# A float32 hybrid decoder layer on one core: planner margins, the gate between attention pairs, the place of the weight loads and of the softplus's rectifier

## The chip, the cores and the metric

The kernel runs on one core of one Trainium2 chip. The metric is the time of one execution on the device in microseconds (us). The core has a matrix engine (TensorE, in the rows PE for matmuls and PEld for weight loads into the array), VectorE (DVE), ScalarE (ACT), GpSimd (POOL) and SyncE (SP), whose queue here issues nearly all DMA transfers.

## The reference

One pre-norm layer with 512 tokens of width 2048, in float32. `h = RMSNorm(x)`; one projection `h @ w_in` gives three groups of heads:

- a: RWKV-7 time mixing, 12 heads of 64: a recurrence over time with data-dependent decay (sigmoids, exponentials, a normalised key), then a group norm and a bonus term.
- b: causal pooling over windows of 2, 4, 8, 16, a 128x128 map and a scale for each of four groups.
- c: stick-breaking attention, 12 heads of 64. Queries and keys are RMS-normalised; `z = q k^T`; the weight of a key is `exp(logsigmoid(z) + sum over the later keys before the query of logsigmoid(-z))`; output is weights times values.

Each branch is multiplied by a SiLU gate from the same projection; the concatenation goes through `w_out` and is added to `x`.

## The kernel before

**Precision and the main stream.** Every big product is made of three matmuls: both operands are split into a rounded part and a rest (`hh`, `hl` for the activations, `wh`, `wl` for the weights), and `three` issues hh*wh, hh*wl and hl*wh into one PSUM tile. The projection has 57 column tiles of 128; the first three are done while the inputs arrive, and `project(n)` does each of the other 54 in two halves of 24 matmuls into a bank named `pj` (two of them). Tile order for pair p of heads: cq, ck, cv, cg (attention), k, r of the next pair, v, ga (RWKV), and four times pu, pg (pooling) at the end. Then the output projection runs into banks named `oacc`, four column blocks of eight halves.

**Weights.** `stream` lists the 140 half tiles of weights. `weights(i)` calls `fetch(i)` and `fetch(i + 1)`; a fetch allocates `raw` (two buffers), issues its DMA on SP, casts it on ACT to `wh` (three buffers) and subtracts on DVE to `wl` (two buffers). It does so under a raised priority (`AHEAD`, 300 places).

**The rest is fill-in.** `rwkv(p)`, `attention(p)` and `pooling(g)` are generators. After every matmul of the main stream `pump` resumes each generator whose due time has passed on the clock of `Pace`, a planner with its own costs that is advanced by each matmul (`pace.now`). `need(tiles, tag, margin)` is due at margin (default `MARGIN` = 2.5) after the later of two things: the planner's ready time of the tiles, and the moment when a PSUM bank of that tag (three `g` banks) has been read. `soon` is due 1.5 before the tiles are ready. So a larger margin puts a step's matmuls behind more matmuls of the main stream. What is written so is a program order; when the program is built, a scheduler gives every engine a fixed queue, by priority (program place, less the raise) among what it holds to be ready, and semaphores do the waiting on the chip.

**Attention of a pair.** `attention(p)` waits for the end of pair p-1 (`done[("att", p - 1)]`), then for cq and ck: square, split, a block sum on TensorE (`qm`), a Newton rsqrt, the scaled q and k. For each head and three groups of key blocks it makes `z` on TensorE, copies it to `w`, masks it on POOL, and forms the softplus: `n` = ln(1 + exp(-|w|)) by three ACT steps, `m` = relu(w) by a fourth (`m` has one buffer), a reversed scan over n + m on DVE, a subtraction and an exponential into `w`. Then come the transposes `wT` of the weights into g banks, their copies `wt` on ACT, and the products `o` into a g bank that is kept until all three column groups are in. `emit_rstd` makes the norm of `x` (bank `rb`), which the first finished tiles wait for.

Of the kernel before, what the change touches and what calls it, by code (L numbers as in the profile page):

```python
# [13 lines left out]
P = 128  # L14
# [203 lines left out]
def hybrid_trunk_kernel(ctx: ExitStack, tc: tile.TileContext, x, xT, w_in, w_out, vecs, consts, up_w, pool_w, out):  # L218
# [21 lines left out]
    def name(s):  # L240
        uid[0] += 1
        return f"{s}_{uid[0]}"
# [17 lines left out]
    def gb(s="g"):  # L260
        return bank("g", s)
# [96 lines left out]
    def emit_rstd():  # L358
        rt = cp.tile([P, 3, 4], F32, name="rt")
        ms, y0, t = rt[:, 0, :], rt[:, 1, :], rt[:, 2, :]  # L360
        dve.tensor_tensor(ms, xsum[:, 0, :], xsum[:, 1, :], ALU.add)
        dve.tensor_scalar(ms, ms, 1.0 / D, RMS_EPS, ALU.mult, ALU.add)
        act.activation(y0, ms, AF.Ln)
        act.activation(y0, y0, AF.Exp, scale=-0.5)
        dve.tensor_tensor(t, y0, y0, ALU.mult)
        dve.tensor_tensor(t, ms, t, ALU.mult)
        dve.tensor_scalar(t, t, -0.5, 1.5, ALU.mult, ALU.add)
        dve.tensor_tensor(y0, y0, t, ALU.mult)
        dg = tmp("dg")
        for i in range(4):  # L370
            dve.tensor_scalar(dg[:, i * P:(i + 1) * P], ident, y0[:, i:i + 1], None, ALU.mult)
        rb = gb("rb")
        pe.matmul(rb, ones_c, dg, start=True, stop=True)
        dve.tensor_copy(out=rstd, in_=rb)


# [34 lines left out]
    def soon(*tiles):  # L411
        return need(*tiles, margin=-1.5)
# [29 lines left out]

    HK = KT // 2

    def split_weights(src):
        raw = wp.tile([P, HK * P], F32, tag="raw", bufs=2, name=name("raw"))
        dma(out=raw, in_=src)
        wh = wp.tile([P, HK * P], F32R, tag="wh", bufs=3, name=name("wh"))
        wl = wp.tile([P, HK * P], F32R, tag="wl", name=name("wl"))
        act.copy(out=wh, in_=raw)  # L450
        dve.tensor_tensor(wl, raw, wh.bitcast(F32), ALU.subtract)
        return wh, wl
# [19 lines left out]
    def fetch(i):  # L472
        if i < len(stream) and i not in fetched:
            with tc.high_priority(offset=AHEAD if i > 1 else 60):
                fetched[i] = split_weights(stream[i])

    def weights(i):
        fetch(i)
        fetch(i + 1)
        return fetched.pop(i)  # L480

    def project(n):
# [71 lines left out]
    def rwkv(p):  # L554
# [18 lines left out]
        mm(av, uph[:, P:2 * P], ad2, True, False)  # L573
        mm(av, upl[:, P:2 * P], ad2, False, True)
        a = sigmoid(av, bias=nvec[:, 6 + p:7 + p])
        yield need(*sqp, tag="g")
        ss = gb("ss")
        block_sum(ss, bone_r, sqp)
        rn = sq
# [233 lines left out]


    def attention(p):
        while p > 0 and not done.get(("att", p - 1)):
            yield None
        qk = []
        for kind, gain, slot in (("cq", nvec[:, 12:13], "aq"), ("ck", vec[:, V_KN:V_KN + 1], "ak")):
            while (kind, p) not in got:  # L820
                yield None
            raw = got.pop((kind, p))
            dst = scratch(slot, kind)
            sq = tmp("qs")
            act.activation(sq, raw, AF.Square)
            sqp = split(sq)
            yield need(*sqp, tag="g")
            ms = gb("qm")
            block_sum(ms, bmean_r, sqp)
            y0, t = newton_rsqrt(ms, RMS_EPS, eps_rms, sq)  # L830
            dve.scalar_tensor_tensor(raw, raw, gain, y0, ALU.mult, ALU.mult)
            dve.tensor_tensor(dst, raw, t, ALU.mult)
            qk.append(dst)
# [3 lines left out]
        act.copy(out=kr, in_=k)  # L837
        klo = tmpr("klo")
        dve.tensor_tensor(klo, k, kr.bitcast(F32), ALU.subtract)
        head = []  # L840
        for h in range(2):
            s = slice(h * HD, (h + 1) * HD)
            other = hi if h == 0 else lo
            q2 = ap.tile([P, T], F32R, tag="q2", name=name("q2"))
            k2 = ap.tile([P, T], F32R, tag="k2", name=name("k2"))
            act.copy(out=q2[s, :], in_=q[s, :])
            dve.tensor_tensor(q2[other, :], q[s, :], q2[s, :].bitcast(F32), ALU.subtract)
            act.copy(out=k2[s, :], in_=k[s, :])
            act.copy(out=k2[other, :], in_=k[s, :])
            kl2 = ap.tile([P, T], F32R, tag="kl2", name=name("kl2"))  # L850
            pool.tensor_copy(out=kl2[s, :], in_=klo[s, :])
            pool.tensor_copy(out=kl2[other, :], in_=klo[s, :])
            blocks = {}
            for segs, width in ((((3, 0),), 512), (((2, 0), (0, 384)), 512), (((1, 0),), 256)):
                yield need(q2, k2, kl2, tag="g")
                z = gb("z")
                for i, off in segs:
                    mm(z[:, off:off + (i + 1) * P], q2[:, i * P:(i + 1) * P], k2[:, 0:(i + 1) * P], True, False)
                    mm(z[:, off:off + (i + 1) * P], q2[:, i * P:(i + 1) * P], kl2[:, 0:(i + 1) * P], False, True)

                d0 = segs[0][0] * P
                nd = len(segs)
                pat = [[0, nd], [-1, P]] if nd > 1 else [[-1, P]]
                diag = lambda t: t[:, d0:d0 + nd * P].rearrange("p (a t) -> p a t", a=nd) if nd > 1 else t[:, d0:d0 + P]
                w = ap.tile([P, width], F32, tag=f"w{segs[0][0]}{h}", name=name("w"))
                act.copy(out=w, in_=z[:, 0:width])
                pool.affine_select(out=diag(w), in_=diag(w), pattern=pat, compare_op=ALU.is_gt, fill=-1e5, base=0, channel_multiplier=1)

                n = ap.tile([P, 512], F32, tag="n", bufs=2, name=name("n"))[:, 0:width]
                m = ap.tile([P, 512], F32, tag="m", bufs=1, name=name("m"))[:, 0:width]  # L870
                act.activation(n, w, AF.Abs)
                act.activation(n, n, AF.Exp, scale=-1.0)
                act.activation(n, n, AF.Ln, bias=1.0)
                act.activation(m, w, AF.Relu)
                yield soon(n, m)
                for i, off in segs:
                    sg = slice(off, off + (i + 1) * P)
                    dve.tensor_tensor_scan(n[:, sg][:, ::-1], n[:, sg][:, ::-1], m[:, sg][:, ::-1], 0.0, ALU.add, ALU.add)
                dve.tensor_tensor(w, w, n, ALU.subtract)
                act.activation(w, w, AF.Exp)  # L880
                for i, off in segs:
                    for j in range(i + 1):
                        blocks[(i, j)] = w[:, off + j * P:off + (j + 1) * P]
            head.append(blocks)
            if h == 0:
                while ("cv", p) not in got:
                    yield None
                vs = got.pop(("cv", p))
                yield need(vs, tag="g", margin=MARGIN + 2.0)
                vt = ap.tile([P, 4, P], F32, tag="vt", name=name("vt"))  # L890
                vps = gb("vps")
                for j in range(4):
                    transpose(vps[:, j * P:(j + 1) * P], vs[:, j * P:(j + 1) * P])
                act.copy(out=vt, in_=vps.rearrange("p (j c) -> p j c", j=4))

        o = None
        for js, width in (((0,), 512), ((1, 3), 512), ((2,), 256)):
            parts = []
            for h in range(2):
                yield need(*head[h].values(), tag="g", margin=MARGIN + 2.0)  # L900
                tps = gb("wT")
                pos = {}
                off = 0
                for j in js:
                    pos[j] = slice(off, off + T - j * P)
                    for i in range(j, 4):
                        transpose(tps[:, off:off + P], head[h][(i, j)])
                        off += P
                home = {(0, 0): "q2", (0, 1): "k2", (1, 0): "kl2", (2, 0): "q2", (2, 1): "k2"}.get((js[0], h))
                wt = ap.tile([P, T], F32, tag=home, name=name("wt"))[:, 0:width] if home else tmp("wt", width)  # L910
                act.copy(out=wt, in_=tps[:, 0:width])
                parts.append(wt)
            yield need(*parts, vt, tag="g" if o is None else None)
            if o is None:
                o = gb("o")
            for j in js:
                for h, s in ((0, lo), (1, hi)):
                    mm(o[s, j * P:T], vt[:, j, s], parts[h][:, pos[j]], j == 0, j == 2)
# [104 lines left out]

    def begin():
        yield need(xsum, tag="g")
        emit_rstd()
        for n in range(NFIRST):
            finish(n, first[n])

# [134 lines left out]
```

## Time and profile before

| | us |
|---|---|
| median of three runs (range) | 1008.57 (1006.39 to 1008.71) |
| the profiled execution, time | 1007.96 |
| the profiled execution, span from first to last instruction | 1006.1 |
| matmul busy in the span | 978.3 |
| weight loads into the array, busy | 786.9 |
| VectorE busy | 662.2 |
| ScalarE busy | 511.6 |
| projection with fill-in, from 42.6 to 825.1 | 782.5 |
| output projection, from 825.1 to the end | 181.0 |

The engines' busy times overlap. Matmuls are pipelined and their ends are modelled: a 128x512 matmul is shown as some 0.39 to 0.40 us long, while the next one starts 0.22 to 0.23 us after it.

### The profile page before, as it was taken

Reading aid. Unit: us, or ns where it says so; the run is one execution under the profiler, and the core shown is the slowest. Engines: PE = TensorE matmul, PEld = TensorE weight load, DVE = VectorE, ACT = ScalarE, POOL = GpSimd, SP = SyncE. Lnnn points to the kernel's source line nnn. Section 1 sums busy time; section 2 is a strip of 40 time slices with the busy share of each in tenths; the row PEclk is TensorE's granted clock in tenths of the full one; section 3 lists DMA queues with packets and bytes.
Section 4 is the critical chain, followed back from the end, with each engine's and each line's share of the span. In section 5 each row is a group of like instructions: output and inputs, shape, how many; then the busy total and the mean of one; then the engine's idle time right before and its main releaser. Section 6 shows DMA issues by size and latency. Waiting matters only on the chain. (4 is left out here: it accounts for less than half of the span.)

```text
span 1006.1 us, 13872 instructions
## 1 busy us (share of the span) xinstructions
PE 978.3 (97%) x5132; PEld 786.9 (78%) x5132; DVE 662.2 (66%) x1249; ACT 511.6 (51%) x838; POOL 140.5 (14%) x204
## 2 busy tenths in 40 slices
PE   8999999999899998999999999999999999999998
PEld 7867876888678886788768887788867888888886
DVE  5369784888849885697947979398864666323232
ACT  5656654756556654647546565466552245221210
POOL 0131211121120302112111111203211010000000
PEclk9999999999999999999999999999999999999999
DMA  9622322132321313223131222313232248624241
GB/s 337 216 90 76 103 85 90 63 111 68 105 84 58 114 65 106 79 84 95 64 121 64 90 89 80 105 63 110 72 106 79 98 145 281 219 87 147 93 138 63
DMA packets 62210, 109.17 MB, mean 109 GB/s; under 512 B 29760, under 2 KB 31168, under 8 KB 62144
## 3 DMA queue, kind: packets, MB, share of 16 engines
q1 hardware_dynamic: 62144, 108.30, 32.1%
q8 instruction: 40, 0.66, 0.3%
q14 instruction: 26, 0.21, 0.1%
HBM read 98.84 MB, written 9.44 MB: 108 GB/s over the span
## 5 line engine op out<-in xcount | busy, mean ns | idle before, releaser
L380 PE MATMUL pj<-hh,wl 128*128 128x512 f32 x864 | 343.7, 398 | 7.8 <-DVE wl L212 7.5
L380 PE MATMUL pj<-hh,wh 128*128 128x512 f32 x864 | 345.8, 400 | 0.1
L380 PE MATMUL pj<-hl,wh 128*128 128x512 f32 x864 | 343.4, 398 | 0.0
L212 DVE TENSOR_TENSOR wl<-raw,wh 128x1024 fp32r<-128x1024 f32 x140 | 174.4, 1246 | 174.6 <-PE oacc L380 86.1
L212 ACT CAST wh<-raw 128x1024 fp32r<-128x1024 f32 x140 | 146.4, 1046 | 205.7 <-PE oacc L380 95.2
L380 PEld LDWEIGHTS pj<-hh,wl 128*128 128x128 f32 x864 | 162.8, 188 | 45.7 <-DVE wl L212 12.4
L380 PEld LDWEIGHTS pj<-hh,wh 128*128 128x128 f32 x864 | 162.8, 188 | 33.6 <-issue 1.8
L380 PEld LDWEIGHTS pj<-hl,wh 128*128 128x128 f32 x864 | 163.0, 189 | 32.6 <-issue 2.2
L380 PE MATMUL oacc<-wl,yh 128*128 128x512 f32 x256 | 100.1, 391 | 0.0
L380 PE MATMUL oacc<-wh,yh 128*128 128x512 f32 x256 | 99.8, 390 | 0.0
L380 PE MATMUL oacc<-wh,yl 128*128 128x512 f32 x256 | 99.7, 390 | 0.0
L212 POOL TENSOR_SCALAR e<-e 128x512 f32<-128x512 f32 x28 | 45.2, 1614 | 197.4 <-ACT e L212 179.4
L380 PEld LDWEIGHTS oacc<-wh,yl 128*128 128x128 f32 x256 | 48.1, 188 | 10.3 <-issue 0.2
L380 PEld LDWEIGHTS oacc<-wl,yh 128*128 128x128 f32 x256 | 48.1, 188 | 10.2 <-issue 0.2
L380 PEld LDWEIGHTS oacc<-wh,yh 128*128 128x128 f32 x256 | 48.1, 188 | 10.0 <-DVE u L212 0.2
L212 POOL TENSOR_TENSOR d<-u 128x512 f32<-128x512 f32 x25 | 29.4, 1176 | 149.3 <-DVE xblk L212 67.6
L212 DVE TENSOR_TENSOR pr<-xblk,nblk 128x60 f32<-128x60 f32 (+8 forms) x180 | 46.5, 258 | 5.0
L212 ACT ACTIVATE e<-e 128x512 f32<-128x512 f32 x50 | 31.5, 630 | 35.7 <-POOL e L212 35.3
L212 DVE TENSOR_TENSOR_SCAN n<-n,m 128x512 f32<-128x512 f32 (+3 forms) x48 | 43.8, 923 | 7.5 <-ACT n L212 7.5
L212 DVE TENSOR_TENSOR xblk<-xblk,pr 128x60 f32<-128x60 f32 (+8 forms) x180 | 39.3, 218 | 5.0
L212 POOL CAST kl<-klo 64x512 fp32r<-64x512 f32 x24 | 19.2, 802 | 150.4 <-DVE klo L212 134.9
L212 ACT ACTIVATE n<-n 128x512 f32<-128x512 f32 (+1 forms) x72 | 39.6, 551 | 0.4
(203 smaller groups left out, 1227.5 us busy)
## 6 DMA issues: line engine op xcount, KB each, us to landing
raw<-in_w_in SPq DMA_DIRECT2D x108, 512.0 KB, 3.4
raw<-in_w_out SPq DMA_DIRECT2D x32, 512.0 KB, 3.4
lt<-in_x SPq DMA_DIRECT2D x8, 512.0 KB
xr<-in_x SPq DMA_DIRECT2D x16, 256.0 KB, 5.5
out<-xr SPq DMA_DIRECT2D x16, 256.0 KB, 4.1
yin<-yd SPq DMA_DIRECT2D x14, 256.0 KB, 4.6
fr<-in_w_in SPq DMA_DIRECT2D x12, 256.0 KB, 6.9
nblk<-s SPq DMA_DIRECT2D x24, 128.0 KB, 3.4
```

The costliest lines, as they stand in the source:

```text
L212: return call(*args, **kw)
L380: pe.matmul(o, lhsT, rhs, start=start, stop=stop)
```

## The change

Nothing is computed differently and no instruction is added or removed; some are written down at other places in the program, and some waits of generators are due later. In the diff below:

- `emit_rstd` becomes a generator: its matmul waits for `dg` with a margin of 4.5, and is counted by the planner.
- The block sum of the first pair's key norm (`ss`) is due 3.0 later; that of each query and key norm (`qm`) 1.5 later; the transposes `wT` 2.0 later (6.5 for 4.5); the products `o` 1.5 later (4.0 for 2.5).
- `weights(i)` also issues the DMA of `raw` for i + 2; the cast and the subtraction stay in the fetch.
- `attention(p)` begins when the score part of pair p-1 is done, and waits for the whole of pair p-1 only ahead of its own scores.
- `m` = relu(w) is written after the wait `soon(n)`, just ahead of the scan.

```diff
@@ emit_rstd
         dg = tmp("dg")
         for i in range(4):
             dve.tensor_scalar(dg[:, i * P:(i + 1) * P], ident, y0[:, i:i + 1], None, ALU.mult)
+        yield need(dg, tag="g", margin=MARGIN + 2.0)
         rb = gb("rb")
-        pe.matmul(rb, ones_c, dg, start=True, stop=True)
+        mm(rb, ones_c, dg)
         dve.tensor_copy(out=rstd, in_=rb)
@@ weights
-    def split_weights(src):
-        raw = wp.tile([P, HK * P], F32, tag="raw", bufs=2, name=name("raw"))
-        dma(out=raw, in_=src)
+    raws = {}
+
+    def load_weights(i):
+        if i < len(stream) and i not in raws and i not in fetched:
+            raws[i] = wp.tile([P, HK * P], F32, tag="raw", bufs=2, name=name("raw"))
+            dma(out=raws[i], in_=stream[i])
+
+    def split_weights(i):
+        load_weights(i)
+        raw = raws.pop(i)
         wh = wp.tile([P, HK * P], F32R, tag="wh", bufs=3, name=name("wh"))
...
-                fetched[i] = split_weights(stream[i])
+                fetched[i] = split_weights(i)
 
     def weights(i):
         fetch(i)
         fetch(i + 1)
+        with tc.high_priority(offset=AHEAD):
+            load_weights(i + 2)
         return fetched.pop(i)
@@ rwkv
-        yield need(*sqp, tag="g")
+        yield need(*sqp, tag="g", margin=MARGIN + (3.0 if p == 0 else 0.0))
         ss = gb("ss")
@@ attention
-        while p > 0 and not done.get(("att", p - 1)):
+        while p > 0 and not done.get(("scores", p - 1)):
             yield None
...
-            yield need(*sqp, tag="g")
+            yield need(*sqp, tag="g", margin=MARGIN + 1.5)
             ms = gb("qm")
...
         dve.tensor_tensor(klo, k, kr.bitcast(F32), ALU.subtract)
+        while p > 0 and not done.get(("att", p - 1)):
+            yield None
         head = []
...
                 act.activation(n, n, AF.Ln, bias=1.0)
+                yield soon(n)
                 act.activation(m, w, AF.Relu)
-                yield soon(n, m)
...
                 act.copy(out=vt, in_=vps.rearrange("p (j c) -> p j c", j=4))
+        done[("scores", p)] = True
...
-                yield need(*head[h].values(), tag="g", margin=MARGIN + 2.0)
+                yield need(*head[h].values(), tag="g", margin=MARGIN + 4.0)
                 tps = gb("wT")
...
-            yield need(*parts, vt, tag="g" if o is None else None)
+            yield need(*parts, vt, tag="g" if o is None else None, margin=MARGIN + 1.5)
@@ begin
-        emit_rstd()
+        yield from emit_rstd()
```

## Rows read from the trace of the kernel before

**Rows 1.** The page's first part: busy us (share of the span) and instructions.
```profile
PE 978.3 (97%) x5132; PEld 786.9 (78%) x5132; DVE 662.2 (66%) x1249; ACT 511.6 (51%) x838; POOL 140.5 (14%) x204
```

**Rows 2.** Waits of PE: us in total, times, longest.
```profile
PE pj L380 <- DVE wl L212: 7.5, 8, 1.8
PE o L380 <- ACT wt L212: 4.4, 4, 1.7
PE wT L384 <- ACT w L212: 3.4, 4, 0.9
PE first L380 <- ACT first L212: 2.6, 1, 2.6
PE rb L373 <- DVE dg L212: 1.3, 1, 1.3
...
PE qm L380 <- DVE sl L212: 0.7, 1, 0.7
PE gm L380 <- DVE amr L212: 0.7, 1, 0.7
PE ss L380 <- ACT sh L212: 0.7, 1, 0.7
```

**Rows 3.** Timeline of PE, third attention pair: start, length, idle before.
```profile
383.80 0.39 PE L380 MATMUL pj<-hh,wh 128*128 128x512 f32 x1
384.03 0.39 PE L380 MATMUL pj<-hl,wh 128*128 128x512 f32 x1
385.21 0.50 PE L380 MATMUL pj<-hh,wl 128*128 128x512 f32 x1 [0.79 <-DVE wl L212]
...
386.71 0.27 PE L384 MATMUL wT<-kon,w 128*128 128x128 f32 x1
387.87 0.55 PE L384 MATMUL wT<-kon,w 128*128 128x128 f32 x3 [0.89 <-ACT w L212]
...
392.00 1.08 PE L380 MATMUL o<-wt,vt 128*64 128x512 f32 x4
```

**Rows 4.** Timeline of PE, first pair's key norm.
```profile
82.38 0.39 PE L380 MATMUL qm<-sh,bmean_r 128*128 128x512 f32 x1
83.52 0.51 PE L380 MATMUL qm<-sl,bmean_r 128*128 128x512 f32 x1 [0.75 <-DVE sl L212]
```

**Rows 5.** Projection matmuls and weight loads that ran before 53.0 us.
```profile
0.00:53.00 53.00, 9.23 (x40) 7.51 (x40) 0.00 (x0) 0.97 0.76 273
```

**Rows 6.** Timeline of PE and DVE, 67.2 to 70.2 us.
```profile
67.50 0.39 PE L380 MATMUL av<-ad,sl 128*128 128x512 f32 x1
68.62 0.50 PE L380 MATMUL ss<-sh,bone_r 128*128 128x512 f32 x1 [0.73 <-ACT sh L212]
69.35 0.49 PE L380 MATMUL ss<-sl,bone_r 128*128 128x512 f32 x1 [0.23 <-DVE sl L212]
69.95 0.50 PE L380 MATMUL pj<-hh,wh 128*128 128x512 f32 x1
...
69.21 0.69 DVE L212 TENSOR_TENSOR u<-pj,rstd 128x512 f32<-128x512 f32 x1
```

**Rows 7.** Waits of SP's queue, the longest line.
```profile
SPq L226 <- DVE wl L212: 636.4, 123, 10.7
```

**Rows 8.** Busy time in stretches: PE, PEld, DVE, ACT, POOL, clock, DMA.
```profile
360.00:390.00 30.00, 28.18 (x128) 22.51 (x127) 28.45 (x75) 15.68 (x28) 3.13 (x7) 1.00 0.22 80
393.40:403.20 9.80, 8.38 (x44) 6.24 (x43) 0.00 (x0) 4.23 (x8) 2.63 (x2) 1.00 0.40 120
```

**Rows 9.** Timeline of ACT and DVE, third pair's last scores.
```profile
383.47 0.42 ACT L212 ACTIVATE m<-w 128x256 f32<-128x256 f32 x1 [1.89 <-DVE n L212]
383.80 1.03 ACT L212 CAST wh<-raw 128x1024 fp32r<-128x1024 f32 x1
...
383.94 1.21 DVE L212 TENSOR_TENSOR wl<-raw,wh 128x1024 fp32r<-128x1024 f32 x1
...
404.43 0.68 DVE L212 TENSOR_TENSOR u<-pj,rstd 128x512 f32<-128x512 f32 x1
...
406.60 0.69 DVE L212 TENSOR_TENSOR y<-o,y 128x512 f32<-128x512 f32 x1 [0.68 <-PE o L380]
```

**Rows 10.** Tile raw in two stretches: DVE busy (count), ACT busy (count).
```profile
0.00:376.50 376.50, 59.59 (x47) 50.50 (x49) 1.00 0.33 111
0.00:384.00 384.00, 60.87 (x49) 51.33 (x50) 1.00 0.33 110
```

**Rows 11.** Timeline of DVE, the last RWKV pair's output.
```profile
848.49 0.69 DVE L212 TENSOR_TENSOR yl<-y,yh 128x512 fp32r<-128x512 f32 x1
```

**Rows 12.** Output-projection matmuls and weight loads that ran before 865.9 us.
```profile
0.00:865.90 865.90, 39.23 (x169) 31.75 (x170) 0.00 (x0) 1.00 0.32 108
```

## Prediction, made before the change was run

> **What bounds the kernel now.** I read the page's first part, then PE's waits, then PE's timeline at each wait, then the queues of the engine that PE waits for. TensorE is the bound: its matmuls cover 978.3 of 1006.1 us, no other engine passes two thirds [rows 1]. Its stream has one order, so a step that isn't ready holds everything behind it, and the change neither adds nor removes an instruction: all it can win is PE's waiting. PE's named waits are few and sort by cause: 7.5 us on the subtraction `wl`, 4.4 on the copies `wt` ahead of `o`, 3.4 on `w` inside `wT`, and single ones of 2.6, 1.3 and some 0.7 [rows 2].
>
> The idle figure understates a wait. Around one, matmuls start 0.23 us apart (383.80, 384.03), and then the next at 385.21: 1.18, so 0.95 lost, where the row says 0.79 idle [rows 3]. The difference, 0.16, is the pipelined tail of the matmul before. So I take idle plus 0.16 a time: `wl` 7.5 + 8 x 0.16 = 8.8, `o` 4.4 + 4 x 0.16 = 5.0, `wT` 3.4 + 4 x 0.16 = 4.0 us. All the waits that the edits aim at, with `rb`, `qm` and `ss` (1.4, 0.9, 1.4), come to 21.5 us or 2.1%. That is the ceiling; the question is which of them an edit reaches.
>
> **`wT`, 2.0 us later.** Four times the first transposes run and those of the last key blocks wait: 386.71, then 387.87 with 0.89 idle [rows 3]; the longest of the four is 0.9 idle [rows 2], 1.06 lost. The four stand together with no projection matmul between them, so the planner's due time put them there, and a due time 2.0 later puts some nine projection matmuls ahead. Those are at hand (their weights come two halves ahead except at the `wl` waits). 2.0 covers 1.06: gain 4.0. Lower bound: 0, if the lateness grows along with the delay; nothing here makes `w` later by itself.
>
> **`o`, 1.5 us later.** The same reading: four waits, 5.0 lost, the longest 1.7 idle or 1.9 lost [rows 2]. 1.5 leaves 0.4 of it and covers the others: gain 4.6, and I take 4.5. Lower bound 0 again.
>
> **`qm`, 1.5 later.** One wait: 82.38 to 83.52 for a 0.23 step [rows 4], 0.9 lost, and covered: gain 0.9. The other eleven pairs of `qm` show next to nothing, so elsewhere this edit only moves the chain.
>
> **`rb`.** PE waits 1.3 idle, 1.4 lost, on `dg` [rows 2]. In the program of before, `rb` stands at the head of the first streamed tile: its generator waits only for `xsum`, and the planner never gives `xsum` a ready time, because the squares write it as `accum_out`, which the planner counts as an input. Yet 40 projection matmuls are ahead of it on the chip [rows 5]. So its place was not the program's but the scheduler's, who held `dg` ready only then. By the planner's costs the new due time is 3.4 us of small operations plus 4.5, some 35 matmuls into the tile: still ahead of where it ran. Gain 0; the other end is 1.4, if the place moves with it. The readers of `rstd` come no later by this reading.
>
> **`ss` of the first pair, 3.0 later.** PE loses 0.9 and 0.5 at it, but the matmul behind it starts at 69.95, and the bank that this one needs is read by `u` from 69.21 to 69.90 [rows 6]. Take `ss` out and PE waits for that read instead. What is late next is the evacuation; its place on DVE is behind the same `sl`. Gain 0, ends -0.5 (the two matmuls of `ss`, 0.46, no longer lie under the wait) and +1.4.
>
> **Weight loads.** For the load to come sooner, a buffer must be free. In 123 cases SP's queue waits for a `wl`, the last reader of the buffer, 636.4 us in all [rows 7]: the loads already leave as their buffer is released, and there are still two. Gain 0. SP has other transfers in that queue (`s1`, `s2`, `lt`, `up`, `yd`); a load that is put ahead of them while its buffer is taken would hold them, at most the longest wait of 10.7 us once, on the RWKV chain and not on PE. The Trainium skill, Perfetto Trace Analysis, section Optimization Strategy, says that the same gap repeating on the engine that should be saturated can mean too few buffers for the next tile. By that rule an earlier issue with two buffers leaves all 8.8 us; by the edit's own idea some would go. Trace and rule agree on the buffer; whether it is what makes `wl` late is the next part.
>
> **The rectifier.** At the last scores of a pair ACT waits 1.89 for the scan before `m` can be overwritten, with the weight cast behind it [rows 9]. If `m` goes behind that cast, the cast comes up to 1.89 sooner. But PE's wait at 384.03 is for the subtraction at 383.94, the 49th, and the 49th cast had begun before 376.5 [rows 10]: it lay ready for six microseconds while DVE worked off its queue. DVE is busy 28.45 of 30 us there, and then 0.00 of 9.8 [rows 8]. So the weight waits are DVE's late queue in the stretch where the scans meet the triangular inverse, and this edit takes nothing off DVE. Gain 0, ends +8.8 (the order changes and all go) and -4 (half as many again).
>
> **The gate.** Pair p's query tile was evacuated at 404.43, the attention of p-1 ended at 406.60 [rows 9]. The later steps move that end by 2.0 for `wT` and 1.5 for each of three `o`, 6.5 us; with the old gate the next norm would wait for it, with the new one it starts some 2 us sooner than before. The scores' own wait costs nothing: `z` needs the key tile, which comes a tile later. Gain 0.
>
> **Sum.** 4.0 + 4.5 + 0.9 = 9.4 us off the profiled execution's 1007.96 (span 1006.1 and 1.9 around it; 0.6 under the median of 1008.57): 998.5 us.
>
> **Rivals.**
> - The weight waits go too. For it: the cast does stand behind the rectifier, and any new order of DVE's queue may put `wl` sooner. Against: [rows 8, 10]. 1007.96 - 9.4 - 8.8 = 989.8. Chance 0.17.
> - The gain is given back. The moved steps run from 393 to some 413 instead of 407, into the start of the next RWKV pair, where `dec`, `av`, `ss` and `q1` use the same banks, DVE and ACT. For it: each engine's queue is fixed beforehand, so a late copy holds others. Against: DVE idles 9.8 us just before [rows 8]. Two new waits of 0.9 (as `qm`) a pair, over five pairs, take back 9: 1007. Chance 0.19.
> - Slower: the RWKV chain runs out of time. `o` keeps one of three g banks from 392.00 [rows 3] to 407.29 [rows 9], now to some 413.8, and the first steps of the next RWKV pair need g banks. If each pair passes the 6.5 on, the last pair is 39 us late. Its output is split at 849.18 [rows 11], and the half that uses it begins with the 169th output matmul, at 865.6 to 865.9 [rows 12]: 16.6 of slack. PE would wait 22.4: 998.5 + 22.4 = 1021. It starts to cost from 2.8 us a pair and makes the kernel slower by more than 0.3% from (16.6 + 13.1) / 6 = 4.9. Against: the planner knows the banks, and 9.8 idle us of DVE can catch a chain up. Chance 0.14.
> - The forecast: the three margins alone. Chance 0.50, its own range 994 to 1004.
>
> **How the numbers follow.** A change of 0.3% (3 us) is about what can be told from none: 1005.5 to 1011.6 is the same. Faster: the first rival (0.17), nearly all of the forecast (0.46) and a third of the giving back (0.06): 0.69. Same: 0.04, 0.10 and the mild end of the slow chain (0.02): 0.16. Slower: 0.12 of the chain and 0.03 of the giving back: 0.15. The range runs from 987 (all waits gone, with `rb` and half of `ss`: 989.8 - 1.4 - 0.7 and 1 for the run) to 1012, which leaves out most of the slow chain and a thin end below.
>
> **What would show it.** Right: PE's waits for `w` and for `wt` fall from 3.4 and 4.4 to under 1 each; the single wait for `qm` goes; `rb` still runs after some 40 matmuls with over 1 us idle, and the matmul after the first pair's `av` still starts near 70; SP still waits for `wl` some 120 times; PE's `wl` waits stay between 5 and 10. Wrong: the `wl` waits are gone, or PE has new waits between 400 and 440 and its like in each pair, or the last pair's `yl` lands after the half that needs it.

## The result and the profile after

The changed kernel takes 1015.69 us (median of 4 runs, 1014.79 to 1017.42), the kernel before in the same series 1008.64. The ratio is 1.0067, 95% interval 1.004 to 1.0093: slower by 7 us, where 10 us less had been forecast. Ratios, here and below, are to the kernel before in the same series. The execution profiled took 1016.01 us, span 1014.2.

The page's first part of the changed kernel:

```profile
PE 983.6 (97%) x5132; PEld 787.9 (78%) x5132; DVE 660.6 (65%) x1249; ACT 511.2 (50%) x838; POOL 144.4 (14%) x204
```

The work is that of [rows 1]; the span is 8.1 us longer. Its waits (total, times, longest), which answer to [rows 2]:

```profile
PE pj L381 <- DVE wl L212: 12.1, 12, 1.8
PE s L381 <- DVE uv L212: 2.0, 3, 1.4
...
PE ss L381 <- ACT sh L212: 1.9, 1, 1.9
PE gm L381 <- DVE bx L212: 1.4, 2, 0.7
PE o L381 <- ACT wt L212: 1.3, 1, 1.3
PE gh L381 <- DVE bx L212: 1.1, 2, 0.8
...
PE tr L385 <- DVE bx L212: 0.9, 3, 0.4
...
PE rb L381 <- DVE dg L212: 0.4, 1, 0.4
...
PE qm L381 <- DVE sl L212: 0.2, 1, 0.2
```

The reader sees two lists in one. What the margins aimed at is gone or small: `wT` (3.4 before) has no row, `o` fell from 4.4 to 1.3, `qm` from 0.7 to 0.2. In their place `wl` rose from 7.5 to 12.1, and `s`, `gm`, `gh` and `tr` of the RWKV chain wait, which hardly did. Measured from each matmul's start to the next one's, and put down to the tile of the first, the steps of `wT` became 4.65 us shorter, of `o` 3.7, of `qm` 0.9; those of `pj` became 8.3 longer, of `gh` 3.5, of `gm` 2.3, of `av` (the wait ahead of `ss`) 1.4.

The stall at 258.17 in PE's timeline, and VectorE's timeline ahead of it (start, length):

```profile
256.26 0.39 PE L381 MATMUL pj<-hl,wh 128*128 128x512 f32 x1
258.17 0.50 PE L381 MATMUL pj<-hh,wl 128*128 128x512 f32 x1 [1.52 <-DVE wl L212]
```
```profile
251.55 0.74 DVE L212 SCALAR_TENSOR_TENSOR d<-d,vec,u 128x512 f32<-128x512 f32 x1
...
254.85 1.21 DVE L212 TENSOR_TENSOR_SCAN n<-n,m 128x512 f32<-128x512 f32 x1
255.98 0.18 DVE L212 TENSOR_TENSOR pr<-xblk,nblk 128x48 f32<-128x48 f32 x1
256.17 0.69 DVE L212 TENSOR_TENSOR w<-w,n 128x512 f32<-128x512 f32 x1
256.77 0.20 DVE L212 TENSOR_TENSOR xblk<-xblk,pr 128x48 f32<-128x48 f32 x1
256.89 1.22 DVE L212 TENSOR_TENSOR wl<-raw,wh 128x1024 fp32r<-128x1024 f32 x1
```

No row has idle time ahead of it: steps of the inverse (`pr`, `xblk`), a scan and its subtraction run without a break, and `wl` has its turn among them. Its cast had ended 8.5 us and its buffer had come free 6.9 us before the subtraction began (both found by following that half's `wh` and the last reader of the buffer). At all twelve stalls of the changed kernel these are 5.6 to 9.6 and 5.6 to 8.5 us; at the ten of before, small ones counted, 6.8 to 8.8 and 5.0 to 7.2. So the data is there, and VectorE's fixed order is what PE waits for.

### The profile page after: what moved, and what is told of

The parts are those of the page before. It is cut to its first block, busy times and chain, and to the rows that moved or that the text cites. A ratio compares the mean times of both kernels' runs of the same rounds, so it can differ in the third digit from the quotient of the medians.

```text
span 1014.2 us, 13863 instructions
## 1 busy us (share of the span) xinstructions
PE 983.6 (97%) x5132; PEld 787.9 (78%) x5132; DVE 660.6 (65%) x1249; ACT 511.2 (50%) x838; POOL 144.4 (14%) x204
## 4 chain that ended last, share of the span: by engine, by line
PE 59%; DVE 20%; issue 8%; ACT 7%; DMA 3%; POOL 2%; SPq 0%; POOLq 0%; DVEq 0%; ACTq 0%
PE pj L381 31%; PE oacc L381 17%; DVE wl L212 5%; DVE bx L212 2%; DVE n L212 2%; DVE xblk L212 2%; DVE pr L212 2%; PE first L381 2%; PE o L381 1%; POOL e L212 1%; ACT n L212 1%; PE wT L385 1%; DVE u L212 1%; DVE w L212 1%; DMA lt<-in_x 1%
## 5 line engine op out<-in xcount | busy, mean ns | idle before, releaser
L381 PE MATMUL pj<-hh,wl 128*128 128x512 f32 x864 | 345.2, 399 | 12.3 <-DVE wl L212 12.1
L212 DVE TENSOR_TENSOR wl<-raw,wh 128x1024 fp32r<-128x1024 f32 x140 | 173.7, 1242 | 158.0 <-PE oacc L381 85.8
L212 DVE TENSOR_TENSOR_SCAN n<-n,m 128x512 f32<-128x512 f32 (+3 forms) x48 | 39.3, 831 | 17.9 <-ACT m L212 9.6
L212 ACT ACTIVATE e<-e 128x512 f32<-128x512 f32 x50 | 31.4, 629 | 34.3 <-POOL e L212 33.8
L212 DVE TENSOR_TENSOR xblk<-xblk,pr 128x60 f32<-128x60 f32 (+8 forms) x180 | 43.5, 242 | 4.6
L212 DVE TENSOR_TENSOR pr<-xblk,nblk 128x60 f32<-128x60 f32 (+8 forms) x180 | 43.3, 241 | 4.7
```

Source lines behind the costliest of these rows:

```text
L212: return call(*args, **kw)
L381: pe.matmul(o, lhsT, rhs, start=start, stop=stop)
```

## The experiments

The runs come in the order in which they were made; a theory that fell is named where it fell. Where the edit is a part of the change, its hunk stands with the change and is only named.

**1. The change without the rectifier's hunk, and that hunk alone.** The suspicion after the result was that a rectifier just ahead of the scan makes the scans late, and the `wl` behind them.

> The changed kernel with the rectifier back at its old place (m written ahead of the wait, the wait for n and m). Late-rectifier theory: in the changed kernel the scan waits 9.6 us on DVE for m, in the stretch where DVE has no slack; without that the scans' wait for m falls under 2 us, PE's wl waits fall from 12.1 to 8 or less, and the time to 1006 to 1010. Redraw theory (every edit redraws the fixed queues, and where waits fall is luck): the wl waits land anywhere from 5 to 13, and the time anywhere from 1003 to 1018, with no tie to the wait for m. Crowding theory (the next pair's norm beside the output half meets the RWKV steps): PE's waits for bx and uv (6 us in the changed kernel) stay, time 1010 to 1015.

> The kernel before with the rectifier's move alone. Late-rectifier theory: scans wait 8 us or more for m, PE's wl waits rise from 7.5 to 11 or more, time 1011 to 1015; the waits for w in wT and wt in o stay, as no margin moved. Redraw theory: time anywhere from 1000 to 1016. Crowding theory: no change beyond 3 us, since the gate is the old one.

Measured: without it 1013.72 us (ratio 1.0033, 1.0018 to 1.0047), `wl` still 11.9; alone 995.07 us (0.9865, 0.983 to 0.9899). PE's waits with the hunk alone:

```profile
PE s L380 <- DVE uv L212: 3.0, 5, 1.3
...
PE pj L380 <- DVE wl L212: 0.6, 1, 0.6
PE o L380 <- ACT wt L212: 0.4, 1, 0.4
PE wT L384 <- ACT w L212: 0.4, 1, 0.4
```

The suspicion falls, and so does "gain 0": the hunk alone nearly empties all three waits with no margin changed. 995 us lies below every range that was named before the run. The third pair's last matmul into `z` ends at 360.5 there, at 374.2 before.

**2. The two later margins with the gate, and a margin that aims at nothing.** The first takes the hunks of `wT`, `o` and the gate alone; the second is

```diff
-MARGIN = 2.5
+MARGIN = 2.6
```

> The kernel before with the two later margins of the attention's output half (wT 2.0, o 1.5) and the new gate, nothing else. My prediction's sum: waits for w and wt fall from 7.8 to under 2, time 1008.5 - 8.5 = 1000. Crowding theory: the same fall, but 4 to 6 us of new waits for bx and uv, time 1004 to 1008. Redraw theory: the fall, and wl waits anywhere from 5 to 13, time 997 to 1010.

> The kernel before with the default margin 2.6 for 2.5: an edit that aims at nothing. Redraw theory: PE's waits move between causes by several us and the time moves by 3 us or more, either way. Late-rectifier and crowding theories: within 3 us of before, the same waits of the same size, as no mechanism of theirs is touched.

Measured: 1010.73 us (1.0018, 1.0002 to 1.0035) and 1012.63 (1.003, 1.0019 to 1.0041). In the first, `wT` and `o` have no row left, and `wl` has 11.3 us and `s` 4.5. So the margins do what they were said to do and earn nothing; the time lies just above all three ranges named for it. The second keeps the waits at their places (`wl` 8.6 and `o` 6.6 are larger, `wT` 2.8 smaller): an edit that aims at nothing, and moves 104 of TensorE's 5132 instructions in their order, makes the kernel 0.3% longer.

**3. Is the rectifier's gain a property of the hunk?** The hunk with that neutral margin; with the margins of `wT` and `o`; with the gate; and half of it, the sooner wait without the later rectifier:

```diff
                 act.activation(m, w, AF.Relu)
-                yield soon(n, m)
+                yield soon(n)
```

> The kernel before with the rectifier edit alone (995.07 us) and, besides, the planner's default margin 2.6 for 2.5, which aims at nothing and cost 0.3% in the kernel before. Theory A, a stretch of VectorE's queue that the rectifier edit relieves: the relief doesn't hang on one order, so 994 to 1000 us, and PE's waits for wl stay under 2.5 us. Rival, a lucky draw of the queues' order: any new order throws it away, 1003 to 1012 us, wl waits 5 to 12.

> The rectifier edit and the two margins of wT and o, no gate. In the run with the rectifier alone PE's waits for w and wt were already 0.4 each, so the margins have nothing left to win. Theory A1, the later last steps crowd the next pair's start by themselves: wl and g-bank waits (s, gm, gh) come back by 4 or more together, 999 to 1006 us. Theory A2, only the gate crowds: 994 to 998 us, wl under 2.

> The rectifier edit and the gate, no margin. Theory A2, the gate crowds (the next pair's norm stands beside the last pair's products and the start of the RWKV pair): wl waits over 5, 1001 to 1009 us. Theory A1, the margins crowd and the gate by itself does nothing: 993 to 998 us, wl under 2. If both e6 and e7 stay under 998, it is the two together or one of the four other edits that costs the gain.

> Half of the rectifier edit: the rectifier stays where it was, ahead of the wait, but the wait is for n alone, so the scans are written down sooner by the planner's cost of the rectifier. If the gain of the whole edit comes from the scans' sooner place, 993 to 999 us and wl waits under 2. If it comes from the rectifier's own place behind other work of ScalarE (a weight cast that no longer stands behind a rectifier which waits for the last scan), 1004 to 1012 us and wl waits 6 to 10.

Measured: 1021.63 us (1.012, 1.009 to 1.0149), 1011.59 (1.0021, 1.0001 to 1.004), 1008.46 (0.9981, 0.9962 to 1.0) and 1013.02 (1.0025, 1.0013 to 1.0038). The first decides: 0.1 us on a margin turns 995 into 1022, by waits at other places:

```profile
PE pj L380 <- DVE wl L212: 6.5, 5, 2.0
PE wT L384 <- ACT w L212: 3.9, 4, 2.9
PE gh L380 <- DVE bx L212: 2.6, 4, 0.8
PE o L380 <- ACT wt L212: 2.5, 1, 2.5
```

Theory A falls, and 1021.63 us lies above its rival's range too. 995 us belongs to one order of the queues, not to the hunk as such. The gain didn't last beside the two margins (past both ranges named) nor beside the gate (1008.46, `wl` 4.5), and the half of the hunk that was run alone doesn't have it.

**4. Less load on VectorE by another engine; the steps sooner; one margin alone.** Every third subtraction goes to GpSimd, in either kernel; `wT` and `o` are due 1.0 sooner; the hunk of `o` stands alone.

```diff
-        dve.tensor_tensor(wl, raw, wh.bitcast(F32), ALU.subtract)
+        eng = pool if i % 3 == 2 else dve
+        eng.tensor_tensor(wl, raw, wh.bitcast(F32), ALU.subtract)
```
```diff
-yield need(*head[h].values(), tag="g", margin=MARGIN + 2.0)
+yield need(*head[h].values(), tag="g", margin=MARGIN + 1.0)
-yield need(*parts, vt, tag="g" if o is None else None)
+yield need(*parts, vt, tag="g" if o is None else None, margin=MARGIN - 1.0)
```

> The kernel before, with the subtraction wl of every third weight half on GpSimd instead of VectorE: 46 times 1.25 us less on VectorE. Theory D, the waits are VectorE's late queue: PE's waits for wl fall from 7.5 to under 4, 997 to 1005 us, while the waits at wT and o (7.8 together) stay within 5 to 10, since ScalarE's copies and the scans' chain set them. Rival R, the places in the queues are a draw and VectorE's load is not the limit: wl waits 5 to 12, 1004 to 1016 us. A third way: GpSimd's slower subtraction is itself late, and wl waits pass 12.

> The changed kernel with the same third of the subtractions on GpSimd. Theory D: with VectorE relieved the margins keep what they win, so wT and o stay under 1.5 together, wl falls from 12.1 to under 4 and the waits of the RWKV steps from 7.5 to under 4: 994 to 1003 us, and 3 to 9 us less than the kernel before with the same relief. Rival R: wl 8 to 14, the RWKV steps 5 to 10, 1008 to 1019 us.

> The kernel before with wT and o due 1.0 sooner instead of later. By the reckoning of the prediction each of the eight waits grows by 1.0 and the shorter ones come in: 1015 to 1026 us. Theory of a debt that only changes its place: the waits at wT and o rise from 7.8 to 12 or more, those for wl and in the RWKV steps fall from 9.5 to under 6, and the time stays at 1005 to 1013 us.

> The kernel before with the margin of o alone 1.5 longer. By the reckoning of the prediction 4.5 us less: 1003 to 1006 us, o under 1. Debt theory: o under 1, but wl or wT or the RWKV steps rise by 3 to 6 together, 1006 to 1012 us.

Measured: 1064.93, 1042.18, 1042.73 and 1011.44 us (ratios 1.0566, 1.0327, 1.0335, and 1.0017 with 1.0004 to 1.003; the second is 2.6% above the changed kernel). With GpSimd nearly every step waits more, and mostly for VectorE. The groups of VectorE and GpSimd (busy, mean ns; idle before them) in the kernel before with this edit show that it is no clean relief:

```profile
L212 DVE TENSOR_TENSOR u<-pj,rstd 128x512 f32<-128x512 f32 x50 | 34.4, 687 | 6.6 <-PE pj L380 6.0
L212 DVE TENSOR_TENSOR w<-w,n 128x512 f32<-128x512 f32 x24 | 20.7, 864 | 1.6
L212 POOL TENSOR_TENSOR wl<-raw,wh 128x1024 fp32r<-128x1024 f32 x46 | 113.0, 2456 | 304.9 <-PE pj L380 127.6 <-PE oacc L380 123.9 <-ACT y L212 21.2
```

Of the 57.6 us of subtractions that left it (174.4 to 116.8), VectorE keeps 43 in longer instructions: its busy time falls from 662.2 to 647.9. `w<-w,n`, which reads two operands that lie in SBUF, takes 864 ns where it took 689; `u<-pj,rstd`, which reads one from PSUM, 687 for 688. So both expectations were tested on a quarter of the relief; theory D's numbers failed all the same. Sooner steps don't wait longer at `wT` and `o` (5.8 for 7.8) but at `wl` (17.1) and in the RWKV steps (15.5); that misses both expectations. Moved either way, sooner here or later in the changed kernel, these steps add waits at `wl`.

The run of `o` alone is what the prediction's step needed. Its waits:

```profile
PE pj L380 <- DVE wl L212: 11.0, 11, 1.9
PE s L380 <- DVE uv L212: 3.0, 5, 1.0
...
PE gm L380 <- DVE amr L212: 1.8, 3, 0.7
PE wT L384 <- ACT w L212: 1.8, 2, 0.9
PE gm L380 <- DVE bx L212: 1.4, 2, 0.7
```

The row of `o` is gone, and with this one line of the change `wl` is at 11.0 and `s` and `gm` wait, as in the changed kernel.

**5. A third buffer for `wl`.** In the fixed order `wl` can't come ahead of its free buffer. The buffer is paid for with two temporaries, so each kernel has a control with these two less:

```diff
-TP = 16
+TP = 14
-        wl = wp.tile([P, HK * P], F32R, tag="wl", name=name("wl"))
+        wl = wp.tile([P, HK * P], F32R, tag="wl", bufs=3, name=name("wl"))
```

> The kernel before with 14 temporaries for 16, the control for the next run. If only the draw counts, 1004 to 1016 us with wl waits of 5 to 12; if temporaries bind, over 1020.

> The kernel before with a third buffer for wl, paid for with two temporaries. Theory Q, the subtraction's place in VectorE's fixed queue is set when its buffer comes free, one half (some 5.5 us) ahead of its use, which is too little where that queue runs 5 to 8 us late: with a buffer a half sooner PE's waits for wl fall from 7.5 to under 2.5, 998 to 1006 us against e13 less 4 to 10. Rival R, a draw: wl waits 5 to 12, no nearer to 998 than e13.

> The changed kernel with 14 temporaries, the control for the next run. 1008 to 1022 us, wl waits 8 to 14.

> The changed kernel with a third buffer for wl and 14 temporaries. Theory Q: wl from 12.1 to under 2.5 while wT and o stay under 1.5: 999 to 1008 us, 8 to 14 less than e15. Rival R: wl 7 to 14, within 5 us of e15 to either side.

Measured: 1009.95 (1.0005, 0.9992 to 1.0017) and 1015.76 us for the controls, which change nothing: the traces show the order of every engine as it was. With the third buffer it is 1015.17 (1.0056, 1.0037 to 1.0075) and 1025.92 (1.0171, 1.0148 to 1.0194), 0.5% and 1.0% above the controls. The waits of the kernel before with the third buffer, and of the changed one:

```profile
PE wT L384 <- ACT w L212: 13.3, 8, 2.6
...
PE o L380 <- ACT wt L212: 2.2, 1, 2.2
```
```profile
PE wT L385 <- ACT w L212: 13.9, 5, 4.3
...
PE pj L381 <- DVE wl L212: 0.9, 1, 0.9
```

Half of theory Q holds: `wl` had too late a place, and a buffer sooner it leaves the list (7.5 to nothing, 12.1 to 0.9). The other half, the time, fails: what `wl` gives up stands at `wT`. In the kernel before, TensorE's order is the control's but for 6 of its 5132 instructions, so this move is made by the queues of the other engines. VectorE at the third pair's last scores, in the control and with the third buffer:

```profile
390.48 0.41 DVE L212 TENSOR_TENSOR w<-w,n 128x256 f32<-128x256 f32 x1
...
391.80 1.23 DVE L212 TENSOR_TENSOR wl<-raw,wh 128x1024 fp32r<-128x1024 f32 x1
```
```profile
392.46 1.21 DVE L212 TENSOR_TENSOR wl<-raw,wh 128x1024 fp32r<-128x1024 f32 x1
393.59 0.41 DVE L212 TENSOR_TENSOR w<-w,n 128x256 f32<-128x256 f32 x1
```

The `wl` of the same half now stands ahead of the last `w`, and PE waits 2.09 us for that `w`, to 394.51. Four of the eight `wT` waits, 9.0 of the 13.3 us, have a `wl` directly ahead in this way.

**6. Work off VectorE with nothing moved.** Every second step of the inverse is left out, so the inverse is not the true one.

```diff
-        for j in range(1, B - 1):
+        for j in range(2, B - 1, 2):
```

> The kernel before, with every second step of the triangular inverse (pr and xblk) left out, so the inverse is not the true one; some 6.5 us a pair less on VectorE, in the stretch where the waits stand, and nothing moved to another engine. Theory D, one debt of VectorE in that stretch: PE's idle time at wl, wT and o together falls from 15.6 to under 6, and the time to 993 to 1001 us. Rival R, a draw of orders with no debt behind it: 10 to 18 idle, 1003 to 1016 us.

> The changed kernel with the same steps of the inverse left out. Theory D: wl, wT and o together from 13.6 to under 6, the RWKV steps stay at some 5 to 8, 1001 to 1009 us, no sooner than e17, since the margins buy nothing that the debt did not hold. By the reckoning of the prediction, whose margins gain once wl no longer takes it back: 3 to 9 us under e17. Rival R: 10 to 18 idle, 1010 to 1021 us.

Measured: 1022.3 (1.0131, 1.0105 to 1.0156) and 1022.12 us (1.0135, 1.0118 to 1.0152), with 36 and 38 us less work on VectorE. Waits of the kernel before, so relieved:

```profile
PE gh L380 <- DVE bx L212: 5.1, 6, 2.0
PE s L380 <- ACT uv L212: 4.2, 2, 2.4
PE tr L384 <- DVE bx L212: 2.7, 1, 2.7
...
PE pj L380 <- DVE wl L212: 1.7, 3, 1.0
```

What theory D said of the three places came: `wl`, `wT` and `o` together fall from 15.6 to 1.7 us. It fails for the time: 24.2 us of waits stand at other steps, mostly RWKV's, which had 1.7. TensorE's order moved as well (1511 of 5132 instructions), so less work and a new order aren't told apart here. The margins win nothing in this setting either, 1022.12 us with them against 1022.3, where the prediction's reckoning asked for 3 to 9 us.

**All runs side by side.** PE's idle gaps in us, summed over each trace by the tile of the matmul behind the gap, between 75 and some 830 us; the last column also has what lies outside. The time is the median; the gaps are those of the profiled execution, which took up to 5.1 us more (rectifier, `wT`, `o` later) or 4.5 less (`wT`, `o` sooner). "Other" is mostly RWKV.

| kernel | time | `wl` | `wT` | `o` | other | all |
|---|---|---|---|---|---|---|
| before | 1008.6 | 7.8 | 3.4 | 4.4 | 1.7 | 23.7 |
| margin 2.6 | 1012.6 | 8.6 | 2.8 | 6.6 | 1.3 | 26.2 |
| 14 temporaries | 1010.0 | 8.1 | 3.5 | 4.9 | 1.8 | 25.6 |
| `soon(n)` | 1013.0 | 7.7 | 2.0 | 6.4 | 3.7 | 27.0 |
| rectifier and gate | 1008.5 | 4.5 | 0.4 | 8.9 | 1.5 | 23.0 |
| third `wl` | 1015.2 | 0 | 13.3 | 2.2 | 2.1 | 24.4 |
| `o` later | 1011.4 | 11.0 | 1.8 | 0.1 | 7.0 | 27.4 |
| `wT`, `o` later, gate | 1010.7 | 11.3 | 0 | 0 | 8.9 | 29.4 |
| rectifier, `wT`, `o` later | 1011.6 | 12.2 | 0 | 0 | 8.7 | 26.8 |
| changed, no rectifier | 1013.7 | 11.9 | 0.5 | 0 | 7.2 | 26.9 |
| changed | 1015.7 | 12.3 | 0 | 1.3 | 7.5 | 26.8 |
| changed, 14 temporaries | 1015.8 | 12.0 | 0 | 1.1 | 8.0 | 27.7 |
| changed, third `wl` | 1025.9 | 1.0 | 13.9 | 1.2 | 11.0 | 33.8 |
| rectifier | 995.1 | 0.7 | 0.4 | 0.4 | 6.4 | 15.0 |
| rectifier, margin 2.6 | 1021.6 | 6.6 | 3.9 | 2.5 | 10.3 | 29.5 |
| half the inverse | 1022.3 | 1.7 | 0 | 0 | 24.2 | 32.3 |
| changed, half the inverse | 1022.1 | 4.4 | 0 | 0 | 20.6 | 31.4 |
| `wT`, `o` sooner | 1042.7 | 17.1 | 5.8 | 0 | 15.5 | 46.6 |
| GpSimd, before | 1064.9 | 12.3 | 0 | 5.2 | 31.5 | 58.2 |
| GpSimd, changed | 1042.2 | 18.4 | 0 | 0 | 14.6 | 40.6 |

In the six kernels with the later `o` and nothing done to `wl`'s buffers or VectorE's load (the rows from `o` later to changed with 14 temporaries), `o` is 0 to 1.3, `wl` 11.0 to 12.3 and other 7.0 to 8.9. `wl` and `wT` taken together are 11.2 us before and 11.3 to 12.7 in these six, 11.4 and 11.5 in the two kernels with margin 2.6 and 14 temporaries, 13.3 with the third buffer. With the rectifier's hunk they are 1.1 alone and 4.9 beside the gate.

## Why the prediction was wrong

**`wT`, `o`, `qm`: the waits themselves went as forecast.** Their steps became 4.65, 3.7 and 0.9 us shorter for 4.0, 4.5 and 0.9. **`rb`:** 0.9 gained for 0. Its place did move with the margin: it runs behind 47 projection matmuls, not 40, and waits 0.4 for 1.3. **`ss`: the wait as forecast.** It grew from 0.7 to 1.9, and the matmul behind it starts at 70.15, before at 69.95. But the granted clock is 0.50 from 70.2 to 73.6, where it was 1.00 before: 1.7 us that the term doesn't have. (The kernel before has such a stretch at 735.3, which the changed one hasn't.)

**Weight loads: right as a rule.** SP still waits on `wl`, 130 times:

```profile
SPq L226 <- DVE wl L212: 677.7, 130, 13.0
```

In the kernel before, half of the loads leave within 0.07 us of their buffer coming free, but seven of 138 leave 2 to 4 us after it; three of these matter for `o`, below. The hunk was not run alone. **The gate:** not run alone either; beside the rectifier it goes with 13 us more than the rectifier alone, which after experiment 3 says little.

**The step that failed is the sum:** gains were added while the waits beside them were held as they were. Two terms carry the failure.

The first is the `wl` waits, held at 8.8 "by VectorE's late queue" while `wT` was to gain 4.0 beside them. The reading of that queue was right, the conclusion was not: `wl` and the subtraction `w` stand in one queue and in one stretch. In the changed kernel `wT` lost its 3.4 us and `wl` gained 4.5; together they went from 11.2 to 12.3. The third buffer shows how these two trade: with TensorE's order kept and `wl` put ahead, `wl` goes to nothing and `wT` from 3.4 to 13.3. The margin of `wT` was not run alone, and the later `o` alone already has `wl` at 11.0 and `wT` at 1.8, so which margin moved how much stays open.

The second is "`o`, 1.5 later: gain 4.5", by "the same reading". `o` had another cause. The kernel before on SP, VectorE, ScalarE and TensorE, at the third pair's products:

```profile
393.01 0.34 SPq L226 DMA_DIRECT2D lt<-s  x1
393.44 1.01 SPq L226 DMA_DIRECT2D raw<-in_w_in  x1
```
```profile
388.27 1.22 DVE L212 TENSOR_TENSOR wl<-raw,wh 128x1024 fp32r<-128x1024 f32 x1
```
```profile
398.07 1.04 ACT L212 CAST wh<-raw 128x1024 fp32r<-128x1024 f32 x1 [2.00 <-DMA raw<-in_w_in]
399.02 1.06 ACT L212 COPY wt<-wT 128x512 f32<-128x512 f32 x2
```
```profile
399.65 1.56 PE L380 MATMUL o<-wt,vt 128*64 128x384 f32 x8 [1.42 <-ACT wt L212]
```

The buffer of that weight load came free with the `wl` at 388.27, but the load stood behind an `lt` of the RWKV chain in SP's queue and left 3.95 us later. The cast waited for it, and the copy `wt` stood behind the cast. Three of the four waits at `o` are of this kind; the fourth copy stood behind two steps `e` that waited for GpSimd. VectorE was idle in the last 3 us before each of the four; the second of the stretches in [rows 8] holds the one shown. So `o` was no part of VectorE's lateness, and the wait at it gave VectorE no time that it had a use for. The margin did hide these waits: alone it takes `o` from 4.4 to 0.1. But `wl` and `wT` together go from 11.2 to 12.7 and the other steps, mostly RWKV's, from 1.7 to 7.0: 6.8 us against 4.3, and the kernel comes out 0.17% longer where 4.5 us were to be won. In that run the third pair's last product stands one half tile of weights later in TensorE's order, beside the first RWKV steps of the next pair. That the crowding there makes the new waits is argued and not shown.

The Trainium skill, Perfetto Trace Analysis, section Optimization Strategy, says that the same gap repeating on the engine that should be saturated can mean too little room for the next tile. For `wl` the run with a third buffer agrees (7.5 to none); for the time it doesn't (0.56% longer).

**The rectifier, "gain 0, takes nothing off DVE".** Wrong as a price of one number: -13.6 us alone, +13 with a margin of 2.6, and some 2 us of cost in the changed kernel (1013.72 without it, in another series). It is not a term that can be added.

**The rivals.** "The gain is given back" is the one that came nearest: new waits in the RWKV steps. They are at `s`, `gm`, `gh` and `tr` more than at `dec` and `q1`, and only some half of what came back; the rest is `wl`, so the time passed its 1007. Its sign, new waits between 400 and 440, came in the changed kernel, with `wl` at 407.0 and `gh` at 432.8. "The weight waits go too" happened in the run of the rectifier alone. The slow chain, decided by the last pair's `yl`, did not: no wait for `yl` stands in PE's list.

**What stays open.** That the waits came back, and where, is shown; why the later `o` brings more of them to `wl` and the RWKV steps than it takes away is not, and the scheduler's own clock is in no trace. The sum of `wl` and `wT` is not fixed by VectorE's work either: with the rectifier's hunk alone it is 1.1 us, and VectorE is busy 657.3 us for 662.2. The idle sums leave part of the changed kernel's 8.1 us unexplained, since they grew by 3.1. The two GpSimd kernels are longer by 56 and 26 us. Of the first's, 34.5 us are idle time, and its mean granted clock is 0.973 for 0.996, 28.7 against 4.0 us of full speed lost. What the slower instructions of VectorE have to do with these waits is measured nowhere. The fastest kernel run is the one with the rectifier's hunk alone, 1.35% under the kernel before; its neighbour with a margin of 2.6 says how little that is worth as a rule.

## What to carry to other kernels

For each wait of the bound engine, look at what stood ahead of the releasing instruction in its own queue, and at what that waited for. Two waits that look alike in the list (`wT` and `o` here) can hang on two engines. Waits that hang on one late engine in one stretch should be counted as one sum: a margin or a buffer that removes one of them can move it to the next. Where queues are fixed when the program is built, price an edit against one that aims at nothing (here a margin of 2.6 for 2.5: 0.3%, and 2.7% beside the rectifier), before its parts are credited with anything. And an edit that empties a wait has only been half read until the list of the waits that were near nothing has been read too.

## What the runs showed of the hardware

Beside a busy GpSimd VectorE's `w<-w,n`, whose two operands lie in SBUF, took 864 ns for 689, and `u<-pj,rstd`, with one operand in PSUM, 687 for 688, in the rows of experiment 4. The subtractions `wl` that were left on VectorE, with two SBUF operands too, took 1242 for 1246 on average, so this run gives no rule for all of them.

A long wait of PE can cost more than its idle time. In the kernel before with a third `wl` buffer, PE's timeline and windows of 2 us (PE busy, granted clock, DMA share, GB/s):

```profile
272.95 0.30 PE L384 MATMUL wT<-kon,w 128*128 128x128 f32 x1 [1.04 <-ACT w L212]
275.86 0.65 PE L384 MATMUL wT<-kon,w 128*128 128x128 f32 x3 [2.61 <-ACT w L212]
```
```profile
272.00:274.00 2.00, 0.30 (x1) 1.00 0.34 131
274.00:276.00 2.00, 0.14 (x1) 1.00 0.26 40
276.00:278.00 2.00, 2.00 (x7) 0.54 0.78 191
278.00:280.00 2.00, 2.00 (x7) 0.61 0.48 136
280.00:282.00 2.00, 2.00 (x10) 1.00 0.77 176
```

After two waits of 1.04 and 2.61 us the granted clock is 0.54 and 0.61, mostly its level of 1.2 GHz: (0.46 + 0.39) x 2 = 1.7 us lost on top. The mean clock of this run is 0.988 for 0.996 before, 12.1 against 4.0 us of full speed lost. So here fewer and longer waits cost more than nearly the same idle time in shorter ones: the idle sum is 0.7 us above that of before, the span 6.1.
